# A hybrid trunk on one core: pairs three and four first in the early stage, side tiles at other steps, the last factor split behind a copy, context state and top outputs later

## The chip, the cores and the metric

The kernel runs on one core of a Trainium2 chip. The metric is the device time in microseconds of one execution. In the text PE is the matrix engine, PEld its weight loads, DVE the vector engine, ACT the scalar engine, POOL the general engine, and SP the engine that issues most of the DMAs. Each engine works through its own list of instructions in order; an instruction waits until the semaphores that it asks for are set, and all that is behind it on its engine waits too.

## The reference

One layer of a diffusion trunk on 2048 latent tokens and 256 context tokens of 1024 features, fp32. Cut to what matters here:

```python
m = silu(c) @ w_ada + b_ada                      # shift, scale, gate rows
hl = rmsnorm(x) * (1 + sc1) + sh1                # latent; context the same with its own rows
q, f_fwd, f_bwd, v, g = split(h @ w_in, 5)       # 1024 -> 5 x 1024, 8 heads of 128
# for both directions: S_t = diag(f_t) S_{t-1} + k_t v_t^T, o_t = S_t^T q_t, in chunks;
# the latent scans start from the state in which the context's scan ends
y = (rmsnorm(o_fwd + o_bwd) * silu(g)) @ w_out
lat = x + g1 * y
u = dwconv3(modulate(rmsnorm(lat)) @ w_up)       # 1024 -> 2 x 2816
lat = lat + g2 * ((silu(u_gate) * u_val) @ w_down)
out = rmsnorm(lat)
```

## The kernel before

A tile is 128 tokens or 128 features. Every fp32 operand of a matmul is kept as two parts, high and low; `split` (L79 to L82) makes them: ACT copies the high part (L80), DVE subtracts it from the source (L81). A product is three matmuls for each slice of 128: high by high, high by low, low by high. One call of `multiply` is twelve matmuls of 512 columns.

The big projections use the seven-product scheme of Strassen and Winograd. Weights of a pair of heads are cut in blocks A11 to A22, the modulated tokens in blocks B11 to B22; sums and differences of them are the factors T1 to T4 on the token side and S1 to S4 on the weight side. The products come in the order B11, B21, T2, T1, T3, B22, T4.

Four stages matter here.

- **`early`** (0 to about 570 us): the context's values, then the projections of values v, gates g and queries q for the second half of the tokens (group 1), then for the first half (group 0). `todo` lists the products in order, first B11 and B21 of the four v pairs `vs` and of two g pairs `gs[0:2]`, then the rest, pair by pair. Factors of group 1 are made as it runs: `unit1_step` transposes tokens (L301, into the PSUM banks of tag tr), modulates them (`hm`, L247 on ACT, L248 on DVE), and `differences` and `put_split` (L452 to L457, L80 and L81) write T1 to T4 into four places of SBUF, `rT1` to `rT4`. T2's place is the one that the v pairs' weights `aside` had before. `gs[2]` loads its raw weights (L588) into the place of tag stg, which the tokens' staging tiles use until then.
- **Side tiles**: `side_tokens(j, now)` prepares four tiles for group 0 beside that: load, norm (L130 on ACT, L75 on DVE, a power on POOL, L132 on DVE), four turns (L139, each of four transposes on PE, into banks of tag tr) with their evictions (L143, 16 a pair of tiles, on ACT), differences (L689 to L694 on DVE), and part DMAs (L684). At the end of group 1 `load_factor` reads the parts back (L758, `fraw`), and splits them into the places of the factors (`rT` and `rB` in the profile).
- **`mixer_scan`** (about 570 to 1190 us): for each head the gates' projections (z, L943 to L945), scans on DVE, scores, state updates (kv, L1150) and outputs (o, L1173 and L1176). In the first half a head also runs the context: `context_state` takes its kv (L1094) and makes the head's first states Sf and Sb (L1096 on ACT, L1097 to L1100 on DVE). The tag kv has one PSUM bank, as have o and tr here; ACT's copy sk (L1158) empties kv after each state update. In the last heads `top_outputs`, `top_scaled` and `top_turned` finish the last tile's outputs of the heads already done: oi (L1268) is a PSUM tile of tag o, DVE adds it to the outputs (L1270), ACT squares and sums (L1272).
- **`mixer_out`** (from 1190 us): the output projection, residual and second norm, tile by tile, ghl being the turned outputs' split. The ConvFFN behind it is not touched.

What sets the order: a clock of steps. Each step is one slice of a product, three matmuls; `at(step, f)` puts f on an agenda, and `tick` runs what is due. In each engine's list instructions stand by the step at which they were asked for, as far as the scheduler finds their operands ready by then; `tc.issue_after(i)` puts an instruction behind i.

Of the kernel before, what the change touches and what calls it, by code (L numbers as in the profile page):

```python
# [15 lines left out]
AF = mybir.ActivationFunctionType  # L16
# [29 lines left out]
def body(ctx, tc, a, out):  # L46
# [206 lines left out]
    def early():  # L253
# [10 lines left out]
        clock, at, run, tick = ticking()  # L264
# [245 lines left out]
        c0 = clock[0]  # L510
# [24 lines left out]
        def product(g, p, n):  # L535
            w, r, s = p.w.pop(LEFT[n]), rhs[n], p.z
            if n in ("B11", "T2"):
                z = s["a" if n == "B11" else "b"] = z_tile("za")
            elif n in ("T1", "T3"):
                z = s["d" if n == "T1" else "c"] = z_tile("zd" if n == "T1" else "zc")  # L540
            else:
                z = s[{"B21": "a", "B22": "d", "T4": "c"}[n]]
            multiply(z, w, r, n[0] == "T" and n != "T4" or n == "B11")
            if n == "B11":
                s["u2"] = half_tile("u2", 7)
                act.activation(s["u2"], z, AF.Copy)
            elif n == "T2":
                dve.tensor_tensor(s["u2"], s["u2"], z, OP.add)
            elif n == "T1":
                s["o"] = half_tile("out", 4)  # L550
                dve.tensor_tensor(s["o"], s["u2"], z, OP.add)
            elif n == "T3":
                dve.tensor_tensor(s["o"], s["o"], z, OP.add)
                finished(g, p, 1, 1, s["o"])
            elif n == "B21":
                finished(g, p, 0, 0, half_tile("out", 4), z)
            else:
                o = half_tile("out", 4)
                dve.tensor_tensor(o, s["u2"], z, OP.add)
                finished(g, p, *((0, 1) if n == "B22" else (1, 0)), o)  # L560

        raw_x = []

        def raw_tiles(x):

# [39 lines left out]
        for p in gs[0:2]:  # L605
            p.first_half(rawp.tile([128, D], F32, name="raw", tag="raw"))
        at(c0 + 21, lambda: gs[2].first_half(lp.tile([128, D], F32, name="raw", tag="stg", bufs=1)))
        for i in (0, 2):
            todo += [(1, p, n) for n in ("B11", "B21") for p in vs[i:i + 2]]
        todo += [(1, p, n) for n in ("B11", "B21") for p in gs[0:2]]  # L610
        todo.append((1, gs[2], "B11"))
# [46 lines left out]
        def side_tokens(j, now):  # L658

            if not side:  # L660
                side.append(hq.tile([128, 4, D], F32, name="side", tag="cxt", bufs=1))
            xs, hs = [[side[0][:, 2 * i + u] for u in range(2)] for i in range(2)]
            if j > 1:
                xs = [p.tile([128, D], F32, name="x", tag=tag, bufs=n) for p, tag, n in
                      (((rawp, "raw", 2), (rawp, "raw", 2)), ((hp, "Sf", 1), (hp, "Sb", 1)))[j - 2]]
            hms = [h.rearrange("p (k n) -> p k n", k=KT) for h in hs]
            sums = [x.rearrange("p (k n) -> p k n", k=KT) for x in xs]
            (a11, a21), (a12, a22), (t1, t4), (t3, t2) = [[h[:, 0:4], h[:, 4:8]]
                                                          for h in (*hms, *sums)]

            def load():
                for u in range(2):
                    t = UT * u + j
                    sp.dma_start(xs[u], a["x"][t * 128:(t + 1) * 128])

            def norm():
                for u in range(2):
                    normalize(xs[u], hs[u], pb)

            def turn(u, g):  # L680
                transpose_mod(xs[u], hms[u], g, ps, A1[0], B1[0], "tr", 2, True)

            def put(i):
                sp.dma_start(part_d[i][:, j], (*hms, *sums)[i])  # L684

            def differences():
                put(0)
                put(1)
                dve.tensor_tensor(t1, a12, a11, OP.subtract)  # L689
                dve.tensor_tensor(t3, a22, a12, OP.subtract)  # L690

            def differences2():
                dve.tensor_tensor(t2, a22, t1, OP.subtract)
                dve.tensor_tensor(t4, a21, t2, OP.subtract)  # L694
                put(2)
                put(3)

            load()
            at(now, norm)
            for i, (u, g) in enumerate(((0, 0), (0, 1), (1, 0), (1, 1))):  # L700
                at(now + 8 + 2 * i, lambda u=u, g=g: turn(u, g))
            at(now + 17, differences)
            at(now + 19, differences2)

        for j in range(UT):
            at(c0 + (44, 76, 106, 136)[j], lambda j=j: side_tokens(j, c0 + 52 + (0, 36, 72, 108)[j]))

        spare = []

# [42 lines left out]
        def load_factor(n, into):  # L752
            if not factor_raw:
                factor_raw.extend([hq.tile([128, 2, UT, 4, 128], F32, name="fraw", tag="cxt", bufs=1), 0])
            raw = factor_raw[0][:, factor_raw[1] % 2]
            factor_raw[1] += 1
            i, kh = [(i, p.index(n)) for i, p in enumerate(PARTS) if n in p][0]
            sp.dma_start(raw, part_d[i][:, :, 4 * kh:4 * kh + 4])  # L758
            f = into()
            for j in range(UT):  # L760
                at(clock[0] + 9 + j, lambda j=j: split(f[:, j, 0], f[:, j, 1], raw[:, j]))
            return f

        def next_factor(n):
# [132 lines left out]
    def mixer_scan():  # L897
# [362 lines left out]
        def top_outputs(hs):  # L1260

            n, t = len(hs), NT - 1
            kv, qb, o, g = [top_part(i) for i in range(4)]
            ss, rs = [gp.tile([128, NH], F32, name=m, tag=m, bufs=2) for m in ("ss8", "rs8")]
            top_rs[hs] = rs
            oi = ps.tile([128, n, 128], F32, name="oi", tag="o")
            for j, h in enumerate(hs):
                pe.matmul(oi[:, j], qb[:, h], Sb[:, h], start=True, stop=True)  # L1268
            r = slice(hs[0], hs[-1] + 1)
            dve.tensor_tensor(o[:, r], o[:, r], oi, OP.add)  # L1270
            for j, h in enumerate(hs):
                act.activation(oi[:, j], o[:, h], AF.Square, accum_out=ss[:, j:j + 1])  # L1272
            rms_scale(rs[:, 0:n], ss[:, 0:n], n, 128)
            for h in hs:
                dve.scalar_tensor_tensor(Sb[:, h], Sb[:, h], decb[:, h, t:t + 1], kv[:, h],
                                         OP.mult, OP.add)
# [62 lines left out]
        def head(g, h):  # L1339
# [3 lines left out]
            def ctx_gates():  # L1343
                for d in range(2):
                    gates(d, h, None, project(weight(g, h, 2 - d), None))
                cv = values(cv_d[h // 2][:, h % 2])
                kd, sd, keys = factors(h, None, None, None, None)
                for dt, f in zip((8, 15, 21), (keys, *context_state(h, kd, sd, cv))):
                    at(clock[0] + dt, f)

            def gate(u):
# [22 lines left out]
            for i, w in enumerate(ahead):  # L1374
                at(clock[0] + 2 + 7 * i, lambda w=w: weight(*w))
            gate(1)
            unit(1, (5, 9, 17, 19, 21, 23) if last else (6, 11, 19, 21, 26, 31))
            if last:
                c = clock[0]
                for k in range(4):  # L1380
# [10 lines left out]
        for g in range(2):  # L1391
            for h in range(NH):
                c = clock[0]
                if g == 1 and h == 0:
                    tok.clear()
                    for kk, n in PLAIN.items():
                        sp.dma_start(block(*kk).bitcast(F32), tok_d[n])
                if g == 1 and h == 2:
                    at(c + 2, lambda now=c + 2: gate1(now))
                if g == 1 and 2 <= h < 6:  # L1400
                    for i in range(2):
                        at(c + 12 + 16 * i, lambda k=2 * (h - 2) + i, t=c + 12 + 16 * i: out_scaled(k, t))
                if g == 1 and h == NH - 2:
                    at(c + 36, lambda: load_top(range(6)))
                    for i, hs in enumerate(((0, 1, 2, 3), (4, 5))):
                        at(c + 44 + 10 * i, lambda hs=hs: top_outputs(hs))
                        at(c + 55 + 11 * i, lambda hs=hs: top_scaled(hs))
                        at(c + 65 + 9 * i, lambda hs=hs: top_turned(hs))
                if g == 1 and h == NH - 1:
                    hs = (NH - 2,)  # L1410
                    at(c + 35, lambda: load_top(hs, range(3)))
                    at(c + 42, lambda: top_outputs(hs))
                    at(c + 50, lambda: top_scaled(hs))
                    at(c + 48, lambda: load_top(hs, (3,)))
                    at(c + 57, lambda: top_turned(hs))
                head(g, h)
# [125 lines left out]
    def mixer_out(c3):  # L1542
# [128 lines left out]
        for t in range(NT - 1, -1, -1):  # L1671
# [15 lines left out]
                next_lat = load_lat(t - 1)  # L1687
            g = gs.pop(0)
            if t == NT - 1:
                residual(0, lat, *g, between={3: lambda: heads(t - 1)})  # L1690
                next_lat = load_lat(t - 1)
            else:
                residual(0, lat, *g, between={KT - 1 if t == NT - 2 else 1: turn} if t else {})
# [569 lines left out]
```

## Time and profile before

| | |
|---|---|
| median of 3 runs | 2696.41 us (2693.84 to 2697.68) |
| the profiled execution | 2694.05 us |
| its span, first to last instruction | 2692.3 us |
| mean granted clock of PE | 0.994 |
| PE busy | 2639.1 us, 98% |
| DVE busy | 2076.6 us, 77% |
| ACT busy | 1195.5 us, 44% |

The profiled execution's own time is 1.75 us above its span. In the views a row gives start and duration in us, the engine, the line, the operation, what it writes and what it reads, and in brackets the idle time of the engine just before it, with the instruction that ended it. "x16" is a run of 16 such instructions. A granted clock of 0.50 is half of PE's full rate.

### The profile page before, as it was taken

What the parts mean: (1) busy time and instruction counts of PE and PEld (TensorE: products, weight loads), DVE (VectorE), ACT (ScalarE), POOL (GpSimd) and SP (SyncE); (2) the same over time, 40 slices, a digit from 0 to 9 for tenths busy, and PEclk for the clock granted to TensorE, in tenths of its full rate; (3) what the DMA queues carried; (4) which work ended last, traced back from release to release, by engine and by line L of the source; (5) the groups of instructions that cost most, each with busy time, mean ns of one, the idle gap of its engine ahead of it and who ended that gap; (6) DMA issues with size and microseconds to landing.
All of it is one profiled execution on the core that took longest, in us unless ns stands there. A gap on an engine that the chain in (4) does not pass through costs nothing.

```text
span 2692.3 us, 42039 instructions
## 1 busy us (share of the span) xinstructions
PE 2639.1 (98%) x15800; PEld 2204.6 (82%) x15800; DVE 2076.6 (77%) x2953; ACT 1195.5 (44%) x2051; POOL 609.9 (23%) x934
## 2 busy tenths in 40 slices
PE   6999999999999999999999999999999999999998
PEld 4787788888888888878887888888888888888887
DVE  4857866667887899878888878876887777578896
ACT  4645534433333333345656444443444444333444
POOL 1000222322222122211112444333433440000001
PEclk9999999999999999999999999999999999999999
DMA  8755665374455665558887323227322225888653
GB/s 331 280 204 197 228 205 179 105 255 139 129 160 187 207 202 180 158 177 291 291 317 272 100 79 94 94 70 290 94 94 71 86 79 162 308 281 285 203 180 133
DMA packets 257915, 498.12 MB, mean 185 GB/s; under 512 B 28192, under 2 KB 141232, under 8 KB 249136
## 3 DMA queue, kind: packets, MB, share of 16 engines
q1 hardware_dynamic: 252992, 486.20, 53.0%
q10 hardware_dynamic: 4720, 9.24, 0.9%
q8 instruction: 124, 2.03, 0.3%
q14 instruction: 79, 0.65, 0.1%
HBM read 335.70 MB, written 159.66 MB: 184 GB/s over the span
## 4 chain that ended last, share of the span: by engine, by line
PE 79%; DVE 4%; DMA 2%; ACT 1%; issue 1%; POOL 1%; POOLq 0%; DVEq 0%; SPq 0%; ACTq 0%
PE z L943 4%; PE z L945 4%; PE z L944 4%; PE y L2077 4%; PE y L2076 4%; PE y L2075 4%; PE zc L1474 3%; PE zc L1476 3%; PE zc L1477 3%; PE zd L1474 3%; PE za L1476 3%; PE zd L1476 3%; PE zd L1477 3%; PE za L1477 3%; PE za L1474 3%; PE y L1578 2%
## 5 line engine op out<-in xcount | busy, mean ns | idle before, releaser
L81 DVE TENSOR_TENSOR w<-raw,w 128x512 fp32r<-128x512 f32 (+1 forms) x286 | 226.2, 795 | 73.5 <-ACT w L80 71.3
L80 ACT ACTIVATE w<-raw 128x512 fp32r<-128x512 f32 (+1 forms) x286 | 186.2, 656 | 216.1 <-PE zd L1477 75.1
L81 DVE TENSOR_TENSOR w<-s,w 128x512 fp32r<-128x512 f32 x195 | 174.4, 899 | 81.9 <-ACT w L80 80.2
L2076 PE MATMUL y<-w,mh 128*128 128x512 f32 x600 | 233.5, 389 | 0.2 <-DVE w L81 0.2
L2077 PE MATMUL y<-w,ml 128*128 128x512 f32 x600 | 233.4, 389 | 0.0
L2075 PE MATMUL y<-w,mh 128*128 128x512 f32 x600 | 233.2, 389 | 0.0
L80 ACT ACTIVATE w<-s 128x512 fp32r<-128x512 f32 x195 | 121.8, 630 | 205.6 <-POOL s L220 74.7
L76 POOL TENSOR_TENSOR rs<-rs,mhalf 128x1 f32<-128x1 f32 (+3 forms) x53 | 58.8, 1113 | 447.7 <-DVE rs L75 447.7
L943 PE MATMUL z<-tok,w 128*128 128x512 f32 x352 | 145.7, 414 | 0.0
L1474 PE MATMUL zc<-rT,w 128*128 128x512 f32 x352 | 137.0, 389 | 1.6 <-DMA rT<-rhs1T 1.6
L945 PE MATMUL z<-tok,w 128*128 128x512 f32 x352 | 138.1, 392 | 0.0
L944 PE MATMUL z<-tok,w 128*128 128x512 f32 x352 | 137.7, 391 | 0.0
L1476 PE MATMUL zc<-rT,w 128*128 128x512 f32 x352 | 136.9, 389 | 0.0
L1477 PE MATMUL zc<-rT,w 128*128 128x512 f32 x352 | 136.9, 389 | 0.0
L219 POOL TENSOR_TENSOR s<-raw 128x512 f32<-128x512 f32 x54 | 90.8, 1681 | 195.5 <-DMA raw<-in_w_up_dram 129.6
L987 DVE TENSOR_TENSOR_SCAN S<-F,d 128x528 f32<-128x528 f32 (+1 forms) x80 | 91.4, 1142 | 54.9 <-ACT F L969 54.8
L2076 PEld LDWEIGHTS y<-w,mh 128*128 128x128 f32 x600 | 112.7, 188 | 24.0 <-DVE w L81 0.6
L2075 PEld LDWEIGHTS y<-w,mh 128*128 128x128 f32 x600 | 112.6, 188 | 23.5 <-ACT w L80 0.3
L2077 PEld LDWEIGHTS y<-w,ml 128*128 128x128 f32 x600 | 112.7, 188 | 23.3
L1476 PE MATMUL za<-rB,w 128*128 128x512 f32 x336 | 130.7, 389 | 0.0
L1477 PE MATMUL za<-rB,w 128*128 128x512 f32 x336 | 130.7, 389 | 0.0
L1474 PE MATMUL za<-rB,w 128*128 128x512 f32 x336 | 130.7, 389 | 0.0
(466 smaller groups left out, 7694.9 us busy)
## 6 DMA issues: line engine op xcount, KB each, us to landing
raw<-in_w_up_dram SPq DMA_DIRECT2D x88, 512.0 KB, 3.5
raw<-in_w_in_dram SPq DMA_DIRECT2D x75, 512.0 KB, 5.1
w<-w SPq DMA_DIRECT2D x32, 1024.0 KB, 5.5
lr<-m SPq DMA_DIRECT2D x49, 512.0 KB, 4.6
m<-r SPq DMA_DIRECT2D x66, 256.0 KB, 3.8
spare<-in_w_ada_dram SPq DMA_DIRECT2D x32, 512.0 KB, 5.0
kq<-stash SPq DMA_DIRECT2D x15, 1024.0 KB, 7.5
og<-stash SPq DMA_DIRECT2D x30, 512.0 KB, 4.9
```

The lines of the kernel that those rows point to most:

```text
L80: i = act.activation(h, src, AF.Copy)
L81: j = dve.tensor_tensor(l, src, h.bitcast(F32), OP.subtract)
L943: pe.matmul(z, w[:, 0, k], h, start=k == 0, stop=False, skip_group_check=True)
L944: pe.matmul(z, w[:, 0, k], l, start=False, stop=False, skip_group_check=True)
L945: pe.matmul(z, w[:, 1, k], h, start=False, stop=k == KT - 1, skip_group_check=True)
L987: dve.tensor_tensor_scan(flat(S[:, d]), flat(F[:, d]), flat(d1[:, 0:ns]), 0.0, OP.mult, OP.max)
L1474: pe.matmul(o, w[:, 0, k], r[:, :, 0, k], start=start and k == 0, stop=False, skip_group_check=True)
L1476: pe.matmul(o, w[:, 0, k], r[:, :, 1, k], start=False, stop=False, skip_group_check=True)
L1477: i = pe.matmul(o, w[:, 1, k], r[:, :, 0, k], start=False, stop=k == 3, skip_group_check=True)
L2075: pe.matmul(z, lh, rh, start=start, stop=False, skip_group_check=True)
L2076: pe.matmul(z, lh, rl, start=False, stop=False, skip_group_check=True)
L2077: pe.matmul(z, ll, rh, start=False, stop=stop, skip_group_check=True)
```

## The change

It alters steps and one order, one destination, and one condition; it adds no work and takes none away. In the early stage the v pairs three and four get their first products before pairs one and two. The four side tiles are loaded, normed and turned at other steps, each turn three steps later behind its norm; the split of factor T4 waits for ACT's copy of the newest first product (`copied`), and seven steps longer. In the heads `context_state` runs 27 instead of 21 steps after the gates. The last head's second unit takes its last four steps three earlier. Top outputs come some steps later, and ACT's Squares there write into the SBUF tile qb, which is read before, instead of into the PSUM tile oi. In the first residual the other heads' work is placed two slices earlier. Lines behind L757 have numbers higher by five afterwards.

```diff
-                act.activation(s["u2"], z, AF.Copy)
+                copied.append(act.activation(s["u2"], z, AF.Copy).ins)
...
-        for i in (0, 2):
+        for i in (2, 0):
             todo += [(1, p, n) for n in ("B11", "B21") for p in vs[i:i + 2]]
...
-                at(now + 8 + 2 * i, lambda u=u, g=g: turn(u, g))
-            at(now + 17, differences)
-            at(now + 19, differences2)
+                at(now + 11 + 2 * i, lambda u=u, g=g: turn(u, g))
+            at(now + 20, differences)
+            at(now + 22, differences2)
...
-            at(c0 + (44, 76, 106, 136)[j], lambda j=j: side_tokens(j, c0 + 52 + (0, 36, 72, 108)[j]))
+            at(c0 + (54, 86, 104, 136)[j], lambda j=j: side_tokens(j, c0 + (62, 92, 118, 176)[j]))
...
+            def part(j):
+                with tc.issue_after(copied[-1]) if n == "T4" else ExitStack():
+                    split(f[:, j, 0], f[:, j, 1], raw[:, j])
+
             for j in range(UT):
-                at(clock[0] + 9 + j, lambda j=j: split(f[:, j, 0], f[:, j, 1], raw[:, j]))
+                at(clock[0] + (16 if n == "T4" else 9) + j, lambda j=j: part(j))
...
-                act.activation(oi[:, j], o[:, h], AF.Square, accum_out=ss[:, j:j + 1])
+                act.activation(qb[:, h], o[:, h], AF.Square, accum_out=ss[:, j:j + 1])
...
-                for dt, f in zip((8, 15, 21), (keys, *context_state(h, kd, sd, cv))):
+                for dt, f in zip((8, 15, 27), (keys, *context_state(h, kd, sd, cv))):
...
-            unit(1, (5, 9, 17, 19, 21, 23) if last else (6, 11, 19, 21, 26, 31))
+            unit(1, (5, 9, 14, 16, 18, 20) if last else (6, 11, 19, 21, 26, 31))
...
-                        at(c + 44 + 10 * i, lambda hs=hs: top_outputs(hs))
+                        at(c + 49 + 16 * i, lambda hs=hs: top_outputs(hs))
...
-                    at(c + 42, lambda: top_outputs(hs))
+                    at(c + 45, lambda: top_outputs(hs))
...
-                residual(0, lat, *g, between={3: lambda: heads(t - 1)})
+                residual(0, lat, *g, between={1: lambda: heads(t - 1)})
```

PE in the early stage, before, at the place of the first side tile's turns (tp are the side turns, side_1138 the normed side tile, za a product's bank, w_1065 the split weights of `gs[2]`, loaded from raw_974):

```order
L520 MATMUL za_1101<-tok_707,w_1032 128x512
L139 MATMUL tp_1237<-ident_94,side_1138 128x128 x4
L139 MATMUL tp_1260<-ident_94,side_1138 128x128 x4
L139 MATMUL tp_1275<-ident_94,side_1138 128x128 x4
L139 MATMUL tp_1296<-ident_94,side_1138 128x128 x4
L517 MATMUL za_1169<-tok_596,w_1065 128x512
L519 MATMUL za_1169<-tok_596,w_1065 128x512
L520 MATMUL za_1169<-tok_596,w_1065 128x512
```

The same place after (the side tile is side_1194 and the product's bank za_1166; the next product, with T2's factor, is za_1187):

```order
L520 MATMUL za_1101<-tok_707,w_1032 128x512
L139 MATMUL tp_1303<-ident_94,side_1194 128x128 x4
L139 MATMUL tp_1318<-ident_94,side_1194 128x128 x4
L517 MATMUL za_1166<-tok_596,w_1065 128x512
...
L520 MATMUL za_1166<-tok_596,w_1065 128x512
L139 MATMUL tp_1338<-ident_94,side_1194 128x128 x3
L517 MATMUL za_1187<-rT2_817,w_1098 128x512
L519 MATMUL za_1187<-rT2_817,w_1098 128x512
L139 MATMUL tp_1338<-ident_94,side_1194 128x128
L139 MATMUL tp_1353<-ident_94,side_1194 128x128 x4
L520 MATMUL za_1187<-rT2_817,w_1098 128x512
```

Two turns instead of four stand ahead of the first product with w_1065, and the other two lie behind its twelve matmuls. On ACT one eviction instead of 16 stands ahead of the split of w_1065. On PE the turns tr_958 of the values (L478) stand at row 297, and stood at row 330.

PE in a context head, before (kv_5404 is the context's kv, z_5363 a gate's projection, o_5422 an output):

```order
L945 MATMUL z_5363<-rB22_2750,w_4902 128x512
L1094 MATMUL kv_5404<-v_5143,kt_5329 128x128 x4
L943 MATMUL z_5363<-rB22_2750,w_4902 128x512
L944 MATMUL z_5363<-rB22_2750,w_4902 128x512
L945 MATMUL z_5363<-rB22_2750,w_4902 128x512
L1173 MATMUL o_5422<-states_5306,qi_5192 128x128
```

After (kv is kv_5441, the output o_5412, and z_5425 the next projection):

```order
L950 MATMUL z_5363<-rB22_2750,w_4902 128x512
L1178 MATMUL o_5412<-states_5306,qi_5192 128x128
L1181 MATMUL o_5412<-v_4986,at_5010 128x128
L1178 MATMUL o_5412<-states_5306,qi_5192 128x128
L1181 MATMUL o_5412<-v_4986,at_5010 128x128
...
L949 MATMUL z_5425<-tok_4498,w_4934 128x512
L950 MATMUL z_5425<-tok_4498,w_4934 128x512
L1099 MATMUL kv_5441<-v_5143,kt_5329 128x128 x4
L948 MATMUL z_5425<-tok_4498,w_4934 128x512
```

The context's kv has moved behind the output and into the next projection, 20 rows on.

PE at the first top outputs, before (oi_11449 and o_11474 share the one bank of tag o):

```order
L945 MATMUL z_11404<-tok_8468,w_11201 128x512
L1268 MATMUL oi_11449<-Sb_4665,top_11368 128x128 x4
L943 MATMUL z_11404<-tok_8470,w_11201 128x512
...
L945 MATMUL z_11404<-tok_8470,w_11201 128x512
L1173 MATMUL o_11474<-states_11379,qi_11231 128x128
L1176 MATMUL o_11474<-v_11065,at_11089 128x128
```

After (oi is oi_11502, and the o before it o_11456):

```order
L1178 MATMUL o_11456<-states_11379,qi_11231 128x128
L1181 MATMUL o_11456<-v_11065,at_11089 128x128
...
L950 MATMUL z_11496<-tok_8472,w_11097 128x512
L1273 MATMUL oi_11502<-Sb_4665,top_11368 128x128 x4
L948 MATMUL z_11496<-tok_8472,w_11097 128x512
```

oi has changed places with that o; the next o stands 63 rows behind oi.

More of the change, by code (lines that the diff above doesn't have):

```diff
@@ L560, in product @@
                 finished(g, p, *((0, 1) if n == "B22" else (1, 0)), o)
-        raw_x = []
+        raw_x, copied = [], []
         def raw_tiles(x):
@@ L1405, in mixer_scan @@
                     for i, hs in enumerate(((0, 1, 2, 3), (4, 5))):
-                        at(c + 44 + 10 * i, lambda hs=hs: top_outputs(hs))
-                        at(c + 55 + 11 * i, lambda hs=hs: top_scaled(hs))
-                        at(c + 65 + 9 * i, lambda hs=hs: top_turned(hs))
+                        at(c + 49 + 16 * i, lambda hs=hs: top_outputs(hs))
+                        at(c + 60 + 11 * i, lambda hs=hs: top_scaled(hs))
+                        at(c + 70 + 7 * i, lambda hs=hs: top_turned(hs))
                 if g == 1 and h == NH - 1:
@@ L1411, in mixer_scan @@
                     at(c + 35, lambda: load_top(hs, range(3)))
-                    at(c + 42, lambda: top_outputs(hs))
-                    at(c + 50, lambda: top_scaled(hs))
+                    at(c + 45, lambda: top_outputs(hs))
+                    at(c + 51, lambda: top_scaled(hs))
                     at(c + 48, lambda: load_top(hs, (3,)))
```

## The prediction

> **What bounds the kernel now.** I read the page first, for the share of each engine in the span.
>
> ```profile
> span 2692.3 us, 42039 instructions
> PE 2639.1 (98%) x15800; PEld 2204.6 (82%) x15800; DVE 2076.6 (77%) x2953; ACT 1195.5 (44%) x2051; POOL 609.9 (23%) x934
> ```
>
> PE works 2639.1 of 2692.3 us. The change takes no matmul away, so all that it can win is PE's idle time, 53.2 us, and the time in which PE runs at a lower clock. The second view is the list of PE's waits: what waited for whom, the total in us, how often, and the longest.
>
> ```profile
> PE mps L354 <- DMA wada<-in_w_ada_dram: 10.4, 8, 4.2
> PE kv L1094 <- ACT sk L1158: 6.5, 7, 0.9
> PE mps L354 <- DVE silp L337: 5.2, 1, 5.2
> PE za L517 <- ACT u L546: 2.9, 1, 2.9
> PE o L1173 <- ACT oi L1272: 2.9, 2, 2.4
> PE za L517 <- ACT w L80: 2.7, 1, 2.7
> PE tp L139 <- ACT side L143: 2.6, 2, 1.9
> PE y L1578 <- ACT ghl L80: 1.8, 1, 1.8
> PE tp L139 <- DVE x L132: 1.8, 2, 0.9
> ```
>
> The two L354 rows are the start of the program, which the change leaves alone. The other seven lie where the change moves something. A wait costs more than its idle time where the clock falls behind it, so the third view is the table by stretch around the dearest place (us; then for PE, PEld, DVE, ACT and POOL the busy time and the count; granted clock; DMA share; GB/s).
>
> ```profile
> 108.00:116.00 8.00, 3.08 (x20) 2.16 (x19) 7.92 (x14) 8.00 (x22) 0.00 (x0) 0.87 0.98 338
> 116.00:120.00 4.00, 2.69 (x6) 1.68 (x7) 3.96 (x7) 2.93 (x6) 0.00 (x0) 0.50 1.06 409
> 120.00:126.00 6.00, 6.00 (x19) 4.74 (x18) 4.94 (x9) 1.12 (x2) 0.00 (x0) 0.65 1.03 413
> 126.00:140.00 14.00, 14.00 (x64) 11.58 (x63) 9.16 (x16) 5.73 (x10) 1.10 (x2) 1.00 0.64 215
> ```
>
> The last row gives the normal pace, 14.00 / 64 = 0.219 us a matmul. From 108 to 126 us PE did 45 of them, 16 side transposes and 29 products of 512 columns. 29 x 0.219 = 6.4 us, and 16 transposes at 0.11 to 0.17 (four of them in 0.66, in the row at 97.81 below) are 1.8 to 2.7. So 18 us held 8.2 to 9.1 us of work, and **9.4 us** were lost, about a third of it by the clock of 0.50.
>
> **Early stage, the side tile's turns (A).** What PE waited for at 116 us had two bounds.
>
> ```profile
> 110.12 5.70 ACT L143 ACTIVATE side<-tp,B,A 128x128 f32<-128x128 f32 x16
> 115.60 0.73 ACT L80 ACTIVATE w<-raw 128x512 fp32r<-128x512 f32 x1
> ```
>
> ```profile
> 103.98 0.52 SPq L443 DMA_DIRECT2D tokB<-stg  x1
> ...
> 107.51 0.33 SPq L588 DMA_DIRECT2D raw<-in_w_in_dram  x1
> ```
>
> ```profile
> raw<-in_w_in_dram SPq DMA_DIRECT2D x1, 512.0 KB, 8.0
> ```
>
> ACT had 16 side evictions in a row ahead of the first weight split, 5.70 us. And the raw weights of that split were issued at 107.51, when the place that they share with stg came free, and landed 8.0 us later, 115.5. Both must come earlier. In the changed order one eviction instead of 16 stands ahead of that split on ACT, the four differences on DVE (L689 to L694) stand behind the split, and six product rows on PE lie between the turns. The raw load: pairs three and four come first, so the place of T2's factors comes free at PE row 268 and not 318, DVE's T2 splits fill its idle time near 92 to 96, and the last stg split stands some 5 us earlier. On SP stg's transfer, the 2 MB of tokB and then raw move with it; raw issued near 102 lands near 110 by the 8.0.
>
> The cost is an order that runs tighter near 90 us:
>
> ```profile
> 96.98 0.77 ACT L247 ACTIVATE hm<-tr,B,A 128x512 f32<-128x512 f32 x1
> ```
>
> ```profile
> 97.81 0.66 PE L478 MATMUL tr<-ident,out 128*128 128x128 f32 x4
> ```
>
> ```profile
> 89.19 0.21 DVE L75 TENSOR_SCALAR rs<-ss 128x1 f32<-128x1 f32 x2
> 90.07 0.76 DVE L132 TENSOR_SCALAR side<-side,rs 128x1024 f32<-128x1024 f32 x1 [0.67 <-POOL rs L76]
> ```
>
> The four transposes at 97.81 wait for the bank that ACT's modulation at 96.98 reads. In the new order they stand 33 rows earlier, due at 97.81 - 33 x 0.219 = 90.6 at the latest. The modulation stands behind stg, T2 and T3 splits that wait for DVE in turn, and DVE now has the two L75 and one L132 there, with their wait of 0.67 for POOL. Going through the new rows by these durations I put the end of the modulation near 91.5 to 92. That is a new wait of 1.4 us (0 to 3, the ends being no wait and twice what I find). The second weight split, behind DVE's three sums L219 to L225, is an estimated 1.0 us late, and the first, together with the turns, 0.5. So A gains 9.4 - 1.4 - 1.0 - 0.5 = **6.5 us**, with ends of 3 and 9.4.
>
> A wait can lower the clock, so I looked at it behind three waits:
>
> ```profile
> 317.00:320.00 3.00, 0.23 (x2) 0.00 (x0) 2.65 (x4) 3.00 (x6) 1.27 (x1) 1.00 0.75 239
> 1134.00:1138.00 4.00, 3.78 (x14) 3.29 (x15) 2.34 (x5) 3.02 (x9) 2.16 (x6) 0.57 0.18 47
> 1208.00:1212.80 4.80, 4.72 (x22) 4.03 (x23) 3.62 (x8) 2.53 (x5) 0.00 (x0) 0.67 1.05 428
> ```
>
> During the 2.9-us wait near 318 it stays 1.00, behind the 2.4-us wait at 1134 it is 0.57, behind 1.8 us at 1208 it is 0.67, which costs 4.80 x 0.33 = 1.6 us. My new wait of 1.4 is shorter than the shortest that shows it, so I charge nothing, and keep 1.6 for the range.
>
> [...]
>
> **Later side tiles (B).** The last waits row, L139 for L132's normalised x, 1.8 us in two, is side tile four. Its turns now stand 23 to 40 rows later, singly between products, so x is ready: **1.8 us** gained (1.5 to 2.1). Behind it on SP its part transfers and two raw loads come some 6 us later; these raws are first summed near 250 us in the new DVE order and land near 247.
>
> **Last split behind the copy (C).**
>
> ```profile
> 316.93 0.63 ACT L80 ACTIVATE rT<-fraw 128x512 fp32r<-128x512 f32 x1 [1.92 <-DMA fraw<-part]
> 317.47 0.61 ACT L528 ACTIVATE out<-out 128x512 f32<-128x512 f32 x1
> 317.99 1.65 ACT L80 ACTIVATE rT<-fraw 128x512 fp32r<-128x512 f32 x3
> 319.55 0.57 ACT L546 ACTIVATE u<-za 128x512 f32<-128x512 f32 x1
> ```
>
> ACT's queue stood still for the T4 load, and the copy of za, whose bank PE's next product needs, came behind the splits. Now the copy goes first and PE's 2.9 us go. T4's factor is used some ten products later, so its splits are covered; if they were not, T4's product would wait at most the 2.6 us from 316.93 to 319.55. I take **2.9** (2.4 to 3.2).
>
> **Context state (D).**
>
> ```profile
> 616.40 0.39 PE L945 MATMUL z<-rB,w 128*128 128x512 f32 x1
> 617.71 0.38 PE L1094 MATMUL kv<-v,kt 128*128 128x128 f32 x1 [0.92 <-ACT sk L1158]
> ```
>
> ```profile
> 617.27 0.38 ACT L1158 ACTIVATE sk<-kv 128x256 f32<-128x256 f32 x1 [3.71 <-DVE Sf L1153]
> 618.90 0.39 ACT L1096 ACTIVATE kb<-kv 128x256 f32<-128x256 f32 x1 [1.25 <-PE kv L1094]
> ```
>
> ```profile
> 617.70:659.70 42.00, 41.10 (x428) 36.27 (x428) 34.50 (x53) 15.40 (x28) 10.10 (x32) 1.00 0.46 142
> ```
>
> kv waits until ACT has copied the kv before it out of the one bank, which ends at 617.65. It costs 617.71 - 616.40 - 0.23 = 1.08 us. In the new order 15 products and four o stand ahead of kv, 15 x 0.219 + 4 x 0.11 = 3.7 us, so PE comes at about 620.3, with 2.7 to spare. 7 x 1.08 = **7.6 us** (7.0 to 8.2). The readers of kv (kb on ACT, L1097 to L1100 on DVE) move with it, behind the scan of the second gate; the bank is next wanted 80 rows later.
>
> **Top outputs (E).**
>
> ```profile
> 1131.46 0.39 PE L945 MATMUL z<-tok,w 128*128 128x512 f32 x1
> 1134.22 0.38 PE L1173 MATMUL o<-states,qi 128*128 128x128 f32 x1 [2.37 <-ACT oi L1272]
> ```
>
> ```profile
> 1132.47 0.28 ACT L1272 ACTIVATE oi<-top 128x128 f32<-128x128 f32 x1 [1.88 <-DMA stash<-sk]
> ```
>
> The Squares wrote into oi, which lies in o's bank, so the next o waited: 1134.22 - 1131.46 - 0.23 = 2.53 us, then 4.00 x 0.43 = 1.72 by the clock of 0.57, and 2.9 - 2.4 = 0.5 at the second group. With the Squares writing to qb and oi placed behind that o, all of it goes, 4.75. In the new order the four Squares, 1.6 us from 1132.47 to 1134.08, where the kernel before has its next ACT operation, stand ahead of ACT's kt copy, and PE's second turn waits for that one bank: 0 to 1.6, I take 1.0. Net **3.75** (2.0 to 4.75).
>
> **The rest.** The last unit's steps come three earlier: the same products in other order, 0 (within 0.5 either way). Heads between step 1 instead of 3 of the first residual moves one row; the wait at L1578 stays.
>
> **Sum.** 6.5 + 1.8 + 2.9 + 7.6 + 3.75 = 22.55. The profiled execution took 2694.05 (its span and 1.75 around it), so 2671.5 by its own time. It lies 2.36 below the median of the runs, 2696.41; against that, **2673.8 us**. With all ends good 9.4 + 2.1 + 3.2 + 8.2 + 4.75 + 0.5 = 28.2, with all bad 3 - 1.6 + 1.5 + 2.4 + 7.0 + 2.0 - 0.5 = 13.8.
>
> **The rivals.**
> First, the raw load stays the bound at 116 us. DMA is at 0.98 to 1.06 of its share from 108 to 126, and the load took 8.0 us for 512 KB, so an earlier issue may land no earlier. Against it: near 100 us, where it would now go, the queues are less full by my reckoning of the issues. A gives nothing: 22.55 - 6.5 = 16.05, 2680.4 us. Chance 0.10.
>
> Second, the waits only move. The bank of kv, the bank of tr and DVE's order are each tight; if A, D and E return at the next reader, B and C are left, 4.7 us: 2691.7. Against it stand D's 2.7 us to spare. Chance 0.07.
>
> Third, slower: in the eight context heads DVE becomes the bound. It is busy 34.50 of 42.00 us, in order; kv's readers now wait in its queue for a kv 3.7 us later, and what is queued behind them (the products for the scores' qp and qi, L1045 and L1052) makes PE wait at the scores. It decides the sign once a head loses over 2.5 us, since 8 x 2.5 = 20 eats the other 15 and the bound below. At 3 us a head: 2696.4 - 15.0 + 24 = 2705.4. For it speaks 82% busy; against it that L1097 now stands behind the scan, so DVE has other work until kv is done. Chance 0.05.
>
> **How the numbers follow.** My forecast has 0.78. About 0.2%, 5.4 us, is what a measurement of this kernel tells from no change. Forecast and first rival are faster: 0.88; the second is within: 0.07; the third slower: 0.05. The range reaches from 2696.4 - 28.2 - 2.6 (how far the fastest run lies below the median) = 2665.6 to 2696.4 - 13.8 + 1.3 (how far the slowest lies above it) = 2683.9, which takes in the first rival too.
>
> **What would show it.** In the profile after: the L1094 row gone from PE's waits, and a head 41 us long; no L546 row at 2.9; no L1272 row; the clock 1.00 from 108 to 126, with the first weight split near 111; a new wait of L478 near 90 us. I am wrong if L517 still waits over 2 us for the weight split, if the heads stay at 42 us, or if waits for DVE appear in them.

## The result, and the profile after

The changed kernel takes 2670.18 us (median of 4 runs, 2668.58 to 2672.23) against 2697.05 us (four runs, 2693.84 to 2700.64; ahead of the prediction there were three of them), a ratio of 0.990 with a 95% interval of 0.9883 to 0.9918: faster by 26.9 us. I had put it at 2673.8. The profiled execution took 2669.86 us with a span of 2668.1, 24.2 less than the span before. Of all the executions below one stands apart, of 8324 us at a mean granted clock of 0.31, in the kernel whose split is tied to the copy at nine steps; the figures there are those of its other three.

To see where the 24.2 us come from, I numbered the matmuls of 512 columns in both traces (there are 9,940 in each, in nearly the same order) and subtracted the start of the k-th in one trace from that of the k-th in the other. The difference changes only where one of the kernels waits or runs slowly, and for some rows where their order differs. In us gained, by stage:

| place (time before) | part | forecast | in the trace |
|---|---|---|---|
| 62 to 140 | A, early stage | 6.5 | 8.57 |
| 140 to 250 | B, later side tiles | 1.8 | 2.58 |
| 300 to 325 | C, T4 behind the copy | 2.9 | 2.45 |
| 325 to 350 | a new wait | none | -2.65 |
| 600 to 900 | D, context state | 7.6 | 8.03 |
| 1100 to 1188 | E, top outputs | 3.75 | 4.50 |
| 1188 to 1215 | end of the mixer | 0 | 3.69 |
| start, and behind 1400 | untouched | 0 | -2.98 |

PE's waits after, the longest, in the columns as before (lines behind L757 are higher by five):

```profile
PE tr L478 <- DVE out L553: 2.5, 1, 2.5
PE zc L1479 <- DMA rT<-rhs1T: 1.8, 1, 1.8
PE tr L301 <- ACT out L479: 1.3, 2, 1.0
PE y L1583 <- ACT ghl L80: 1.0, 1, 1.0
PE zc L468 <- ACT cxt L80: 0.8, 1, 0.8
PE zc L470 <- DVE w L81: 0.7, 1, 0.7
PE zc L469 <- DVE cxt L81: 0.7, 2, 0.4
PE za L517 <- ACT w L80: 0.7, 1, 0.7
...
PE za L517 <- ACT u L546: 0.5, 1, 0.5
```

Of the seven rows that the change touched, those for sk, oi, side and x are gone. The wait for the weights has fallen from 2.7 to 0.7, that for u from 2.9 to 0.5, that for ghl from 1.8 to 1.0. The first row is new. The table by stretch over the early stage, and over two context heads:

```profile
108.00:116.00 8.00, 7.32 (x40) 5.67 (x39) 4.77 (x8) 6.15 (x15) 0.00 (x0) 1.00 1.04 346
116.00:120.00 4.00, 4.00 (x19) 3.30 (x18) 4.00 (x8) 4.00 (x11) 0.00 (x0) 1.00 0.99 374
120.00:126.00 6.00, 6.00 (x29) 4.95 (x28) 6.00 (x11) 2.59 (x5) 0.00 (x0) 1.00 0.65 207
```

```profile
607.00:647.90 40.90, 40.90 (x431) 36.37 (x429) 34.44 (x53) 15.41 (x29) 9.72 (x32) 1.00 0.46 145
647.90:688.80 40.90, 40.90 (x431) 36.37 (x430) 34.45 (x53) 15.41 (x29) 9.72 (x32) 1.00 0.46 146
```

From 108 to 126 us PE now does 88 matmuls where it did 45, and the clock stays at 1.00. A head fills 40.90 us without a gap.

### The profile page after: what moved, and what is told of

The parts are those of the page before. It is cut to its first block, busy times and chain, and to the rows that moved or that the text cites. A ratio compares the mean times of both kernels' runs of the same rounds, so it can differ in the third digit from the quotient of the medians.

```text
span 2668.1 us, 42055 instructions
## 1 busy us (share of the span) xinstructions
PE 2632.3 (99%) x15800; PEld 2202.6 (83%) x15800; DVE 2075.6 (78%) x2953; ACT 1195.8 (45%) x2051; POOL 604.9 (23%) x934
## 4 chain that ended last, share of the span: by engine, by line
PE 88%; DVE 4%; DMA 4%; issue 1%; ACT 1%; POOL 0%; SPq 0%; POOLq 0%; DVEq 0%; ACTq 0%
PE z L948 5%; PE z L950 5%; PE z L949 5%; PE y L2081 4%; PE y L2082 4%; PE y L2080 4%; PE zc L1479 3%; PE zc L1481 3%; PE zc L1482 3%; PE zd L1482 3%; PE za L1482 3%; PE zd L1479 3%; PE zd L1481 3%; PE za L1481 3%; PE za L1479 3%; PE kv L1155 2%
## 5 line engine op out<-in xcount | busy, mean ns | idle before, releaser
L1479 PE MATMUL zc<-rT,w 128*128 128x512 f32 x352 | 137.7, 391 | 1.8 <-DMA rT<-rhs1T 1.8
L1479 PE MATMUL za<-rB,w 128*128 128x512 f32 x336 | 130.7, 389 | 0.0
```

Source lines behind the costliest of these rows:

```text
L1479: pe.matmul(o, w[:, 0, k], r[:, :, 0, k], start=start and k == 0, stop=False, skip_group_check=True)
```

## The experiments

All kernels but one are the changed one with a part taken back or altered; the one is the kernel before with a single edit. Times are medians of four runs (five for that one), ratios are to the kernel before. Runs of one kernel spread over 3 to 8 us, so where a part is worth less, I read it from the traces, by the numbered matmuls against the changed kernel's, at the place itself.

### What the last split behind the copy did

T4's split as before:

```diff
-                with tc.issue_after(copied[-1]) if n == "T4" else ExitStack():
+                with ExitStack():
...
-                at(clock[0] + (16 if n == "T4" else 9) + j, lambda j=j: part(j))
+                at(clock[0] + 9 + j, lambda j=j: part(j))
```

> The changed kernel with T4's split as before (nine steps, not tied to the copy). In the changed kernel the 2.9-us wait for ACT's copy (L546) is gone, but a new one of 2.5 us stands at L478 near 335 us. Theory: T4's later splits hold the place that the ada weights (spare) load into, so DVE's rows for the ada sums (L732) come later and DVE finishes L553 too late for PE's turn. Then here the wait at L478 goes, the one for L546 is back, and the time is within 0.6 us of the changed kernel's, 2670. Rival: the wait at L478 comes from the side tiles' later steps. Then it stays here beside the 2.9, and the time is about 2672.7.

Measured: 2670.23 us, ratio 0.9903 (0.9889 to 0.9918). At 300 to 312 us 3.3 us are lost: the wait for L546 (2.2 us) is back, and the clock is 0.57 over the 4 us behind it. At 325 to 340 us 2.65 us are gained, since L478 does not wait. Part C gained nothing on balance, as the theory had it. But PE comes to L478 3.3 us later here, and L553 ends only 2.4 us ahead of it, so this run does not show that DVE would have been in time for an earlier PE.

Tied to the copy, at nine steps:

```diff
-                at(clock[0] + (16 if n == "T4" else 9) + j, lambda j=j: part(j))
+                at(clock[0] + 9 + j, lambda j=j: part(j))
```

> The changed kernel with T4's split tied to the copy as in the change, but at nine steps again instead of sixteen. Theory: the copy stays ahead of the splits, they run right behind it, the spare loads start some 2 us sooner, and both waits are gone or under 1 us: 2667.5 to 2668.5. Rival, that the tie alone already makes the loads late: L478 still waits 2 us or more, 2670.

Measured: 2666.04 us, ratio 0.9887 (0.9871 to 0.9904). L478 does not wait, and L546 costs no more than the 0.5 us of the changed kernel: 2.5 us are gained at 325 to 340 us and nothing is lost before. This version is the best of the three, 4.1 us below the changed kernel by the medians of two separate comparisons, whose intervals overlap. The place shows the gain, the times alone don't settle it.

DVE's rows and SP's loads show the chain. In the changed kernel, the last T4 low splits, the first sum of the ada rows, the first L553, and the loads that the sum waits for:

```profile
309.22 6.89 DVE L81 TENSOR_TENSOR rT<-fraw,rT 128x512 fp32r<-128x512 f32 x4
...
319.98 0.75 DVE L734 TENSOR_SCALAR acc<-spare,sil 128x1024 f32<-128x1024 f32 x1 [2.67 <-DMA spare<-in_w_ada_dram]
...
334.30 0.68 DVE L553 TENSOR_TENSOR out<-out,zc 128x512 f32<-128x512 f32 x1
```

```profile
316.14 1.76 SPq L721 DMA_DIRECT2D spare<-in_w_ada_dram  x4
```

With the tie at nine steps:

```profile
308.30 4.69 DVE L81 TENSOR_TENSOR rT<-fraw,rT 128x512 fp32r<-128x512 f32 x4
...
316.55 1.05 DVE L734 TENSOR_SCALAR acc<-spare,sil 128x1024 f32<-128x1024 f32 x1 [0.66 <-DMA spare<-in_w_ada_dram]
...
331.58 0.67 DVE L553 TENSOR_TENSOR out<-out,zc 128x512 f32<-128x512 f32 x1
```

```profile
313.01 1.76 SPq L721 DMA_DIRECT2D spare<-in_w_ada_dram  x4
```

The spare tile has the place of fraw (both tag cxt), so SP's loads go out just as the last low split ends: 309.22 + 6.89 = 316.11, then 316.14; 308.30 + 4.69 = 312.99, then 313.01. DVE's first sum follows 3.4 us later in the changed kernel, and of the seven sums behind it, 1.2 us each, six stand ahead of the first L553, between the rows for PE's banks. So L553 comes 2.7 us later, and PE waits 2.5 us for it. With the tie at nine steps L553 ends at 332.25 and PE takes up L478 at 332.40, with hardly anything to spare.

The wait at L478 is no accident of one execution. It stands, with 2.2 to 3.0 us, in all nine kernels here that have the tie and the sixteen steps, and in no other. In six of the nine the clock also fell behind it (to 0.63 over 4 us in the kernel with the ada sums later, below), and the place lost another 1.2 to 1.7 us against the changed kernel's own trace, which is one of the other three, with the clock at 1.00 from 335 to 339 us. Against the trace of the kernel before, part C as built comes out even within 0.3 us in these three, and loses 0.9 to 2.2 us in the six.

Sixteen steps without the tie:

```diff
-                with tc.issue_after(copied[-1]) if n == "T4" else ExitStack():
+                with ExitStack():
```

> The changed kernel with the sixteen steps, but T4's split not tied to the copy. Theory: the step alone puts the splits behind the copy, so nothing changes, both the missing wait at L546 and the new one at L478: 2670 within 0.5. Rival: without the tie the splits stand ahead of the copy again, and 2.5 us or more come back at L517: 2672.7.

Measured: 2671.07 us, ratio 0.9907 (0.9892 to 0.9922). My theory fell: the wait for L546 is back with 2.6 us. The step alone leaves the four high splits ahead of the copy; only the tie puts the copy first. L478 does not wait, but only since PE has lost 3.7 us before it: L553 ends at 335.20, and PE takes up L478 at 337.34.

The ada sums' agenda eight steps later:

```diff
-                    at(clock[0] + 16 + 7 * m, lambda: next(rest, None))
+                    at(clock[0] + 24 + 7 * m, lambda: next(rest, None))
```

> The changed kernel with the ada sums' agenda eight steps later and the rest as changed. Theory: the wait at L478 is DVE's queue, in which the rows L732 stand ahead of L553; with them later L553 is in time and 2.5 us go: 2667.6. Rival: DVE is late there for other reasons (weight splits), the wait stays: 2670.

Measured: 2672.95 us, ratio 0.9916 (0.9899 to 0.9932), L478 waiting 2.3 us. The expectation failed. DVE's first sum starts at the same time as before the edit:

```profile
319.73 0.75 DVE L734 TENSOR_SCALAR acc<-spare,sil 128x1024 f32<-128x1024 f32 x1 [2.52 <-DMA spare<-in_w_ada_dram]
```

It waits for its load, not for its step, so this edit did not move what I meant to move. That DVE's sums are the reason is shown by the pair above and not by this run. The time that this kernel loses against the changed one lies elsewhere: a fallen clock behind L478 (0.63 over 4 us), and a new wait of 2.7 us for ACT's copy (L546) near 515 us.

### Which half of the early edits counts

Pairs one and two first again:

```diff
-        for i in (2, 0):
+        for i in (0, 2):
```

> The changed kernel with pairs one and two first again, side tiles at the new steps. The early stage gained 8.6 us from 108 to 126. Theory: the order of the pairs brings T2's place, the staging tile and with it the raw load of the next weights forward; without it raw lands near 115 again and PE waits there although the evictions are out of the way: 3 to 6 us lost, 2673 to 2676. Rival: the 16 evictions alone were the cost; then under 1 us is lost, 2670.5.

Measured: 2677.36 us, ratio 0.9933 (0.9916 to 0.9949). From 108 to 117 us 8.8 us are lost, the whole of part A and more than I expected.

Side tiles at the old steps:

```diff
-                at(now + 11 + 2 * i, lambda u=u, g=g: turn(u, g))
+                at(now + 8 + 2 * i, lambda u=u, g=g: turn(u, g))
...
-            at(c0 + (54, 86, 104, 136)[j], lambda j=j: side_tokens(j, c0 + (62, 92, 118, 176)[j]))
+            at(c0 + (44, 76, 106, 136)[j], lambda j=j: side_tokens(j, c0 + 52 + (0, 36, 72, 108)[j]))
```

> The changed kernel with the side tiles at the old steps, pairs three and four first. Theory: raw lands early, but 16 evictions in a row stand ahead of the weight split on ACT again, and PE waits 3 to 4 us there; besides the two waits of 1.0 us for the fourth side tile (L132) come back, in all 5 to 7 us, 2675 to 2677. Rival: only the raw load mattered in the early stage; then only the two waits for L132 come back, 2672.5.

Measured: 2671.36 us, ratio 0.9916 (0.9901 to 0.993). In the early stage nothing is lost; the rival is right. At 140 to 235 us 4.0 us are lost in the trace, which is that of the slowest of the four executions (2676.46): the two waits for x, and another for a weight split. The first of the two waits in the second row is the early one of 0.7 us, which the changed kernel has too.

```profile
PE tp L139 <- DVE x L132: 2.2, 2, 1.3
PE za L517 <- ACT w L80: 1.6, 2, 0.9
```

ACT shows why. With the old pairs the split stands behind all 16 evictions, with the old side steps behind one. First the kernel with the old pairs, then the one with the old side steps:

```profile
109.75 5.68 ACT L143 ACTIVATE side<-tp,B,A 128x128 f32<-128x128 f32 x16
115.22 0.73 ACT L80 ACTIVATE w<-raw 128x512 fp32r<-128x512 f32 x1
```

```profile
111.06 0.45 ACT L143 ACTIVATE side<-tp,B,A 128x128 f32<-128x128 f32 x1
111.41 0.63 ACT L80 ACTIVATE w<-raw 128x512 fp32r<-128x512 f32 x1
```

So it was the order of the pairs, not the turns' steps, that put the split ahead of the evictions. Their raw loads, in the same order:

```profile
107.16 0.33 SPq L588 DMA_DIRECT2D raw<-in_w_in_dram  x1
```

```profile
102.36 0.33 SPq L588 DMA_DIRECT2D raw<-in_w_in_dram  x1
```

The kernel before with the pairs' order alone:

```diff
-        for i in (0, 2):
+        for i in (2, 0):
```

> The kernel before with one edit of the change alone: pairs three and four first. With side tiles at new steps and the pairs as before the early gain was gone, and with the side tiles as before and the pairs changed it was there. Theory: the order of the pairs alone frees T2's place, brings the raw load of the next weights 6 us forward and, with it, the first weight split ahead of all but one of the 16 evictions: 8 to 9 us gained from 108 to 126, 2688. Rival: it needs the changed turns as well (both undone the split is late); then under 4 us are gained, 2693 or more.

Measured: 2687.72 us, ratio 0.9969 (0.9956 to 0.9982). Its trace is level with the changed kernel's from 108 to 140 us, so the one edit gains all of the 9.1 us that lie between 108 and 117 us of the changed kernel (part A is less by 0.5 that the changed order loses before that). Its raw load is issued at 102.88 and split at 111.93, behind one eviction, and the wait ahead of that product is 0.68 us, as in the changed kernel.

```profile
102.88 0.33 SPq L588 DMA_DIRECT2D raw<-in_w_in_dram  x1
```

```profile
111.59 0.45 ACT L143 ACTIVATE side<-tp,B,A 128x128 f32<-128x128 f32 x1
111.93 0.63 ACT L80 ACTIVATE w<-raw 128x512 fp32r<-128x512 f32 x1
```

### Context state, top outputs and the last head

The context state at its old step, 21 behind the gates:

```diff
-                for dt, f in zip((8, 15, 27), (keys, *context_state(h, kd, sd, cv))):
+                for dt, f in zip((8, 15, 21), (keys, *context_state(h, kd, sd, cv))):
```

> The changed kernel with context_state 21 steps after the gates again. Theory: the seven waits of 0.92 us for ACT's copy sk are back, each 1.08 us in PE's pace, and nothing else of the change has to do with them: 7.6 to 8.1 us lost, 2678. Rival: the heads are bound by DVE as well, and part of the gain came from other edits; then under 5 us are lost, 2675 or less.

Measured: 2677.69 us, ratio 0.9936 (0.9921 to 0.9951), 7.5 above the changed kernel, and 7.98 between 600 and 900 us by the numbered matmuls. The waits are back, as many and as long:

```profile
PE kv L1099 <- ACT sk L1163: 6.4, 7, 0.9
```

Squares into oi again, at the new steps:

```diff
-                act.activation(qb[:, h], o[:, h], AF.Square, accum_out=ss[:, j:j + 1])
+                act.activation(oi[:, j], o[:, h], AF.Square, accum_out=ss[:, j:j + 1])
```

> The changed kernel with the Squares writing into the PSUM tile oi again, top outputs at the new steps. Theory, that the place of oi decides (it stands behind its o now, and the next o comes 63 rows later): nothing is lost at the first group, 2670 within 0.7. Rival, that the bank decides wherever oi stands: the next o waits for the Squares again, 2.5 us and a lowered clock, 2672.5 to 2674.

Measured: 2667.84 us, ratio 0.9892 (0.9878 to 0.9907). Between 1100 and 1165 us PE waits for nothing, and 0.45 us are gained. With oi behind its o the wait for oi stays away whatever the Squares write into. The gain is a wait of the changed kernel that is missing here:

```profile
PE tr L1080 <- ACT kt L1082: 0.5, 1, 0.5
```

This row stands in all ten kernels with the new place and the new target. With the old target ACT takes its kt copy between the second and the third Square, and PE does not wait. So beside the new place the new target costs half a microsecond.

Old steps, Squares into qb (the steps of `top_scaled` and `top_turned`, not shown, go back as well):

```diff
-                        at(c + 49 + 16 * i, lambda hs=hs: top_outputs(hs))
+                        at(c + 44 + 10 * i, lambda hs=hs: top_outputs(hs))
...
-                    at(c + 45, lambda: top_outputs(hs))
+                    at(c + 42, lambda: top_outputs(hs))
```

> The changed kernel with the top outputs at their old steps, so that oi stands ahead of its o again, but with the Squares still writing into qb. Theory, that the place of oi and the target of the Squares each take away the wait: the bank is free once DVE has added oi (L1270, which ended 1.7 us ahead of the Squares before), so the next o waits 0.7 us or less, and 0.5 to 1.5 us are lost against the changed kernel, 2671. Rival, that only the place counts: o waits 2 us or more and the clock falls, 3.5 to 4.5 us lost, 2674.

Measured: 2671.92 us, ratio 0.9908 (0.9892 to 0.9925). PE's waits from 1100 to 1165 us:

```profile
PE o L1178 <- DVE top L1275: 1.6, 2, 1.3
```

About 1.7 us are lost there, without the clock falling: behind the longer wait the products of 512 columns take 0.39 to 0.40 us from the second on, as they do ahead of it. That lies between what I had expected and the rival: the target alone shortens the wait from 2.4 to 1.3 us and keeps the clock; only the place takes it away. DVE's addition comes behind a scan (1.25 us) and two state updates (0.59 us), which I had not counted.

The last head's second unit at its old steps:

```diff
-            unit(1, (5, 9, 14, 16, 18, 20) if last else (6, 11, 19, 21, 26, 31))
+            unit(1, (5, 9, 17, 19, 21, 23) if last else (6, 11, 19, 21, 26, 31))
```

> The changed kernel with the last head's second unit at its old steps (17, 19, 21, 23). From 1175 to 1215 us of before the changed kernel gained 4.6 us that I had put at nothing. Theory: the earlier unit takes the states' and outputs' transfers out of the way of the gates' and of the output loads on ACT's and SP's queues, so the chain to ghl is 1.5 us shorter, and PE's clock is not lowered: without it 3 to 5 us are lost, 2673 to 2675. Rival: the gain comes from heads between the slices of the first residual, and here nothing is lost, 2670.

Measured: 2670.38 us, ratio 0.9911 (0.9896 to 0.9925), no difference by the times; my theory of 3 to 5 us failed. From 1165 to 1190 us the trace is 1.8 us behind the changed kernel's, about half of the gain in question. PE's waits there:

```profile
PE y L1583 <- ACT ghl L80: 1.8, 1, 1.8
PE oi L846 <- DMA kq<-stash: 0.4, 1, 0.4
PE tp L885 <- DVE og L871: 0.3, 1, 0.3
```

They are three of the four waits that the kernel before has there (L1578, L841, L880); the changed one has a single wait of 1.0. The transfers of the gate q, with the old steps and then in the changed kernel, in median us to landing:

```profile
stash<-q ACTq DMA_DIRECT2D x3, 64.0 KB, 5.3
```

```profile
stash<-q ACTq DMA_DIRECT2D x3, 64.0 KB, 3.6
```

They land 1.7 us sooner when the last unit's own transfers come earlier; that these were in the way is argued from the order of ACT's queue. The other kernels bear the pair out. With the old steps (three kernels) the median is 5.3 to 5.6 us, with the new ones (eleven) 3.4 to 4.3. The waits at L846 and L885, 0.6 to 0.9 us together, stand in the three and in none of the eleven. The wait for ghl does not divide them: 1.7 to 1.8 us with the old steps, 1.0 to 1.8 with the new. Where the clock stayed at 1.00, the place takes 1.8 us longer than in the changed kernel with the old steps, and up to 0.85 us longer with the new. So the earlier unit is worth about 1 to 1.8 us.

The heads' work behind slice three again:

```diff
-                residual(0, lat, *g, between={1: lambda: heads(t - 1)})
+                residual(0, lat, *g, between={3: lambda: heads(t - 1)})
```

> The changed kernel with the other heads' work in the first residual behind slice three again. Theory that the earlier last unit alone gained the 4.6 us at the end of the mixer: nothing is lost here, 2670 within 0.5. Rival, that the place of the heads' work did it: 3 to 5 us are lost, 2673 to 2675.

Measured: 2667.15 us, ratio 0.9899 (0.9882 to 0.9915); by the numbered matmuls 0.3 us are lost there. The edit does next to nothing.

What remains of the 3.69 us at the end of the mixer is the clock. Before, it was 0.67 over 4.8 us behind L1578's wait of 1.8 us, and stayed 1.00 behind the 1.0 us after:

```profile
1182.80:1186.80 4.00, 4.00 (x25) 3.40 (x26) 3.79 (x8) 2.65 (x5) 0.00 (x0) 1.00 1.04 426
```

This is not due to the change. The kernel before with the pairs' order alone, which differs from it over 1000 us earlier, waits 1.7 us here with the clock at 1.00, and is 1.8 us ahead of it at this place. And the kernel with T4's split as before, which differs from the changed one 860 us earlier, waits 1.7 us here and has a clock of 0.71 over the next 4 us. So about half of the 3.69 us is the clock's, which either kernel can lose or keep.

## Why the prediction was right, point by point

**A.** Mechanism right in the main. The raw load was issued at 101.54 (I had reckoned near 102) and split at 110.57:

```profile
98.00 0.53 SPq L443 DMA_DIRECT2D tokB<-stg  x1
100.53 0.32 SPq L652 DMA_DIRECT2D tokB<-tok  x1
101.54 0.33 SPq L588 DMA_DIRECT2D raw<-in_w_in_dram  x1
```

The first rival, that the load would land no earlier, is out: it took 8.2 us, against 8.0 before, and landed 6 us sooner. The prediction gave the raw load to the pairs' order and did not say which edit moves the evictions; my expectation ahead of the run with the old side steps gave them to those steps, and that failed. The pairs' order lifted both bounds. Mis-sized was the new wait near 90 us, 1.4 in the sum. PE waited 0.1 us for the end of ACT's modulation:

```profile
90.44 0.76 ACT L247 ACTIVATE hm<-tr,B,A 128x512 f32<-128x512 f32 x1
```

```profile
91.25 0.66 PE L478 MATMUL tr<-ident,out 128*128 128x128 f32 x4
```

The modulation ended at 91.20, 0.3 to 0.8 us earlier than I had reckoned, and PE came at about 91.1 instead of 90.6. The second weight split, 1.0 in the sum, cost no wait; the first, 0.5 in the sum, cost 0.7. The 1.6 us that the range kept for the clock were not needed: from 62 to 140 us of the changed kernel PE's longest wait is 0.7 us, and the clock is 1.00 throughout.

**B.** Right: 2.58 for 1.8. I had counted idle time alone; in PE's pace each wait costs 1.05, worked out as for kv, which makes 2.1; the other 0.5 us I have not assigned.

**C.** The step that failed is "its splits are covered". I asked when the factor T4 is used, and not who waits for what its splits read. That place is the ada loads', and through them and DVE's queue PE lost 2.65 us where it had gained 2.45. The tie by itself keeps the gain; the seven steps beside it took it away.

**D.** Right: 8.03 for 7.6, with seven waits gone. The third rival is out: DVE is busy 34.44 of 40.90 us, and no PE wait for it appears in the heads that was not there before.

**E.** Right: 4.50 for 3.75. I had charged 1.0 for ACT's kt copy behind the Squares; the wait was 0.5 us. The clock of 0.57 is gone with the wait, as the sum had it. The sum gave the gain to the place and the target together; the place alone takes the wait away.

**The rest.** "The same products in other order, 0" was wrong for the last unit: about 1 to 1.8 us, by its transfers, which I had not followed into the queues of ACT and SP. The heads between slices were rightly put at nothing. The gain of 3.69 there and the losses of 2.98 at places that no edit touches nearly cancelled, and what C lost took back most of what A, B, D and E gained beyond the sum. That the sum of 22.55 came within 1.7 us of the trace's 24.2 is in this part luck. The second rival, that the waits only move, came true at one place, C.

## What to carry to other kernels

When a reader is moved later, ask not only when its result is used but what place its source holds, and which load waits for that place. Where two causes end at the same moment, as the raw load and the 16 evictions did at 115.5 us, one edit may lift both; undoing each edit by itself, and making it alone in the kernel before, tells it. Gains of 1 to 3 us in 2670 are read by numbering the matmuls of two traces and subtracting, since the times of single runs spread over more than that.

## What the runs showed of the hardware

In these traces the clock fell behind some waits of less than 3 us and stayed at 1.00 behind others. Behind PE's wait of 1.8 us for rT (L1479) it was 0.61 over 4 us in the changed kernel:

```profile
1428.40:1432.40 4.00, 4.00 (x11) 3.19 (x12) 1.65 (x2) 2.83 (x3) 0.10 (x1) 0.61 0.97 409
```

Before, it was 1.00 behind a wait of 1.6 us at the same place:

```profile
1455.50:1459.50 4.00, 3.93 (x17) 3.29 (x18) 2.77 (x4) 3.08 (x3) 0.10 (x1) 1.00 0.98 412
```

And in the kernel with the tie at nine steps it was 1.00 behind 1.9 us. The place cost the changed kernel 1.29 us that no edit put there. After the first 60 us the fourteen traces have 41 waits of PE of 1.4 to 3.0 us that begin at a clock of 1.00: in or within 4 us behind 20 of them the clock fell, for 21 it did not. The shortest with a fall is 1.68 us, the longest without one 2.96. So a wait of about 2 us at PE cost these kernels another 1.2 to 1.7 us, or nothing, and a forecast of the next edit to them should charge it with that range.
